# Two small tiles made larger in a one-core decoder layer, and the addresses that move with them

## The chip, the cores and the metric

The kernel runs on one core of a Trainium2 chip. A core has TensorE (matmuls, with a separate step that loads the stationary operand, called weights here), VectorE, ScalarE, GpSimd and SyncE, which work in parallel and wait for each other by semaphores, and 16 DMA engines. SBUF, its working memory, has 128 partitions; the address of a tile is its byte offset within each partition. PSUM takes the results of matmuls. The metric is the device time of one execution, in microseconds (us).

## The reference

One layer of a decoder on a sequence of 512 tokens of 1024 channels, in float32:

```python
cs = silu(c)
mod = cs @ w_ada + b_ada                 # six vectors of 1024
shift1, scale1, gate1, shift2, scale2, gate2 = split(mod)
h = rmsnorm(x, norm1_g) * (1 + scale1) + shift1
qa, ka, va, qd, kd, vd, ga, gd = split(h @ w_in)
out_a = sliding_window_attention(qa, ka, va)     # 8 heads, window 128, sinks
out_d = diff_attention(qd, kd, vd)               # 4 heads, two softmax maps each
merged = sigmoid(ga) * (out_a @ w_branch_swa) + sigmoid(gd) * (out_d @ w_branch_diff)
x = x + gate1 * (merged @ w_out)
h2 = rmsnorm(x, norm2_g) * (1 + scale2) + shift2
x = x + gate2 * conv_ffn(h2)                     # w_up, causal conv, GELU gate, w_down
out = rmsnorm(x, final_g)
```

## The kernel before

Every large product is made of three products in a reduced float32 format. An operand is split into a high part (a cast on ScalarE) and a low part (the rest, a subtraction on VectorE), and TensorE adds high × high, high × low and low × high into one PSUM bank. Where the weights are W and the other operand is h, a step is therefore Wh·hh, Wh·hl and Wl·hh; `mm3` (L131) issues these three. In the names of the profile a matmul reads as out<-moving,weights: `a<-hTA,w0h` has the weights w0h and moves hTA.

Tiles come from pools. A pool lays its buffers one behind another in the order in which the program first asks for them; a tag with `bufs=n` has n buffers in turn. A float32 tile of [128, N] takes 4N bytes of each partition, rounded up to 32. Pools that are closed give their space to the next ones, and a tile that is written over an older one's space waits for the last reader of that one.

Two stages are touched.

**The early loop** (`for gi in range(KT)`, L483, in manual order on VectorE, ScalarE and TensorE). It goes over the eight blocks k of 128 input channels. For each k it makes the modulation of the block (`ac_ops` and `ac_first` sum w_ada times cs on VectorE and ScalarE, `reduce_mod` sums over partitions on TensorE, L328, and `finish_mod` writes two columns into a small tile `mod`), then the normalised, transposed and modulated block hT (`h_turn`, `h_tile`, `h_low`), and `mm_k` (L396) adds the block to six PSUM banks: the first 768 columns of w_in, as 6 blocks of 128, times three products, 18 matmuls with 128x512 moving elements for each k. The third product (`part` 2, high weights, low hT) of k is issued behind the reduction and transposes for k + 1. The weights of the block, w0h and w0l, are tiles of [128, 768]. `split_hi` (L355) takes them from pool w for even k and from pool p1 for odd k:

```python
pl, nb = (wp, WB) if k % 2 == 0 else (pp, 2)
```

In pool p1 the last tiles asked for are, in order: three buffers of mod, two of hf, two of ac, two of w0h, and then two of w0l and two more of ac (ac's two parities have a tag each). mod has [128, 16], 64 bytes a buffer. With the sizes before, hf, ac and the odd weights begin 128 bytes past a multiple of 512. The weights of even k, in pool w, and those of all later projections (also pool w) begin at multiples of 512, and so does each block of 128 columns in them.

**The merge** (from L1096). `add_gate_d` computes the second gate of a block j of 128 channels (weights wgd, 8 × 3 matmuls), and `add_merge` the differential branch: w_branch_diff for two blocks at a time is loaded, split into the tile wbd (`gpart(3, ...)`, pool mlp), and 4 × 3 matmuls of 128x512 moving elements into bank pB use it. The units are queued as gate j, branch j − 1, and at the end branches 6 and 7 follow each other; then the output projection begins (`out_step`, L1452; its weights are the merged tiles mg, its moving tiles wo).

In pool mlp stand, in order: five buffers of gx and those of mg, tdall (buffer gT2), m2, c2, and behind c2 the buffers gT3 (wbd, then two weights of the up projection, then a row of the MLP's hidden activations), gT0 (normalised x, then others), gT1 (the same), gT4 (the first gate's row, then m5w, weights of one product of the up projection) and small statistics. c2 has [128, 40], 160 bytes. With the sizes before, everything behind it down to gT4 begins 160 bytes past a multiple of 512. c2 itself holds shift and scale of the second norm as columns: `turn_m2` (L1140) writes it, and the modulation of the second norm reads it.

Behind the merge come the output projection, the second norm, the up projection with convolution and GELU (L1390 and others) and the down projection (L2045), all with weights in pools w, big and the first tiles of mlp, but for m5w (24 matmuls with 256 moving columns) and the transposes of normalised x (L1496).

Of the kernel before, what the change touches and what calls it, by code (L numbers as in the profile page):

```python
# [8 lines left out]
F32 = mybir.dt.float32  # L9
# [5 lines left out]
P = 128  # L15
# [45 lines left out]
def kernel(  # L61
# [26 lines left out]
    def pool(name, bufs=1, space=None, stack=ctx):  # L88
        kw = {} if space is None else {"space": space}
        return stack.enter_context(tc.tile_pool(name=name, bufs=bufs, reuse_waits="tile", **kw))  # L90
# [128 lines left out]
    pp = pool("p1", stack=p1)  # L219
# [110 lines left out]

    def finish_mod(k, pa):
        pa = pa if k == 0 else [pa[:, 0], pa[:, 1]]
        m = pp.tile([P, 16], F32, tag="mod", bufs=3, name=f"mod{k}")
        last = nc.vector.scalar_tensor_tensor(
            m[:, 0:1], pa[0][:, 0:1], bsc1[:, k : k + 1], n1g[:, k : k + 1], ALU.add, ALU.mult
        )
        if k:
            nc.scalar.activation(m[:, 1:2], pa[1][:, 0:1], AF.Identity, bias=bsh[:, k : k + 1])
        else:
            nc.vector.tensor_add(m[:, 1:2], pa[1][:, 0:1], bsh[:, k : k + 1])  # L340
        mods[k] = m
        return last
# [131 lines left out]
    for j in range(2):  # L474
        nc.tensor.matmul(pa0[j], a0[j], ones, start=False, stop=True)
    turn(3)
    finish_mod(0, pa0)
    split_hi(0, 0)
    keep_warm(2)
# [3 lines left out]
    for gi in range(KT):  # L483
# [24 lines left out]
        if more:  # L508
            if gi == 0:
                split_lo(1, 0)  # L510
            pa = reduce_mod(gi + 1, early_mod(1) if gi == 0 else None)
            if gi == 0:
                mm_k(0, 0, FIRST[5:])
            if ALONE <= gi + 2 < KT:
                ac_first(gi + 2, 1)
                ac_first(gi + 2, 0)
            if gi:
                h_turn(gi + 1)
            last_mod = finish_mod(gi + 1, pa)
            if gi:  # L520
                split_lo(gi + 1, 0)
            split_lo(gi + 1, 1)
            h_tile(gi + 1)
# [572 lines left out]
    bp = pool("mlp")  # L1096
# [32 lines left out]
        units.append((load, branch))  # L1129

    m2 = bp.tile([40, P], F32, name="m2")
    c2 = bp.tile([P, 40], F32, name="c2")
    s2c, a2c = c2[:, 0:8], c2[:, 8:16]
    nc.sync.dma_start(m2[16:32, :], b_ada[0, 3 * D : 5 * D].rearrange("(a p) -> a p", p=P))
    nc.sync.dma_start(m2[32:40, :], norm2_g[0].rearrange("(a p) -> a p", p=P))
# [965 lines left out]
```

## Time and profile before

| | |
|---|---|
| median of 3 runs | 685.16 us (684.44 to 686.75) |
| the profiled execution | 685.38 us, of which the span of instructions is 683.6 |
| mean granted TensorE clock | 0.997 of full |
| early loop after k = 0, 19.3 to 55.5 us | TensorE busy 36.20 of 36.20 us, VectorE 33.34, ScalarE 26.41 |
| second gates and branches, 247 to 305 us | TensorE busy 58.00 of 58.00 us, VectorE 42.17, ScalarE 19.11 |
| TensorE's weight loads | 582.2 us, overlapping the matmuls |

In the profile's groups, a row has line, engine, operation, names, shapes and count, then busy time in us, the mean duration of one in ns, and the idle time before. In the view of one tile or line, a row has the count and then the least, the median and the largest duration in ns, and the first and last start in us. The timeline has start and duration in us. The end of a matmul is modelled by the profiler and overlaps the next one's start, so a duration of 0.39 us does not say that the next matmul starts 0.39 us later: the distance between starts does. Starts are shown to 0.01 us, so distances are best taken over many instructions.

### The profile page before, as it was taken

How to read it: one execution, taken by the hardware profiler on the slowest of the kernel's cores; microseconds unless marked ns; L12 is line 12 of the kernel's file. 1: busy time of each engine (PE TensorE's matmuls, PEld its weight loads, DVE VectorE, ACT ScalarE, POOL GpSimd, SP SyncE). 2: the span in 40 equal slices, each digit the busy share in tenths (PEclk: the TensorE clock that was granted, in tenths of full speed). 3: DMA queues.
4: the chain of work that ended last, by engine and by line, in shares of the span. 5: the costliest groups of instructions: out<-in, count | busy, mean ns of one | idle time of the engine just before them, and what ended most of it. 6: DMA issues, size and time to landing. Idle time of an engine off the chain costs nothing. (4 is left out here: it accounts for less than half of the span.)

```text
span 683.6 us, 10903 instructions
## 1 busy us (share of the span) xinstructions
PE 673.7 (99%) x4005; PEld 582.2 (85%) x4005; DVE 562.5 (82%) x1075; ACT 398.1 (58%) x722; POOL 98.4 (14%) x119
## 2 busy tenths in 40 slices
PE   8999999999999999999999999999999999999995
PEld 5887887878888888888899999999999998888885
DVE  4999875988796756794589988988888999979997
ACT  6776774546543223233377756666666776656765
POOL 3000000011022011021030101112111102440300
PEclk9999999999999999999999999999999999999998
DMA  9995422565466885469644788886879848995903
GB/s 304 351 301 175 144 62 65 161 167 163 142 159 179 254 245 164 163 187 340 204 89 108 174 195 206 185 184 190 213 163 217 207 146 203 201 204 144 167 1 123
DMA packets 117141, 123.87 MB, mean 181 GB/s; under 512 B 5063, under 2 KB 94184, under 8 KB 117088
## 3 DMA queue, kind: packets, MB, share of 16 engines
q1 hardware_dynamic: 97246, 95.11, 44.2%
q0 software_dynamic: 19648, 27.79, 24.3%
q8 instruction: 31, 0.51, 0.3%
q10 hardware_dynamic: 194, 0.28, 0.1%
q14 instruction: 22, 0.18, 0.1%
HBM read 118.97 MB, written 2.11 MB: 177 GB/s over the span
## 5 line engine op out<-in xcount | busy, mean ns | idle before, releaser
L1390 PE MATMUL up<-t,m_whi 128*128 128x256 f32 x512 | 93.5, 283 | 0.1
L1390 PEld LDWEIGHTS up<-t,m_whi 128*128 128x128 f32 x512 | 79.8, 192 | 0.8 <-ACT up L1427 0.3
L1390 PE MATMUL up<-t,m_wlo 128*128 128x256 f32 x256 | 72.4, 283 | 0.0
L953 POOL DMA_DIRECT2D arow<-arow x28 | 22.5, 802 | 249.1 <-DVE sd L822 123.2
L1390 PEld LDWEIGHTS up<-t,m_wlo 128*128 128x128 f32 x256 | 49.1, 192 | 0.0
L1373 PE MATMUL up<-bhl,p_whi 128*128 128x512 f32 x136 | 48.9, 399 | 0.0
L1272 POOL DMA_DIRECT2D s<-in_w_up_dram x21 | 26.9, 1352 | 144.2 <-DMA s<-in_w_up_dram 65.8
L1302 ACT CAST m_whi<-s 128x1024 fp32r<-128x1024 f32 x31 | 32.6, 1052 | 23.8 <-PE up L1390 10.3
L1306 DVE TENSOR_TENSOR m_wlo<-s,m_whi 128x1024 fp32r<-128x1024 f32 x31 | 37.9, 1221 | 6.0 <-ACT m_whi L1302 5.5
L945 DVE SCALAR_TENSOR_TENSOR arow<-ra,cs,arow 128x512 f32<-128x512 f32 x56 | 41.7, 747 | 0.6
L1377 PE MATMUL up<-bhl,p_wlo 128*128 128x256 f32 x136 | 38.3, 281 | 0.0
L1390 PE MATMUL up<-bhl,p_whi 128*128 128x256 f32 x192 | 35.1, 283 | 0.0
L1390 PE MATMUL up<-t,p_whi 128*128 128x256 f32 x176 | 32.1, 283 | 0.0
L1373 PEld LDWEIGHTS up<-bhl,p_whi 128*128 128x128 f32 x136 | 25.6, 188 | 5.5
L1390 PEld LDWEIGHTS up<-bhl,p_whi 128*128 128x128 f32 x192 | 30.0, 192 | 0.0
L817 ACT ACTIVATE sd<-sd,dmx 128x128 f32<-128x128 f32 (+3 forms) x32 | 17.7, 556 | 17.2 <-DVE dmx L807 17.2
L1390 PEld LDWEIGHTS up<-t,p_whi 128*128 128x128 f32 x176 | 27.4, 191 | 0.4
L1390 PE MATMUL up<-bhl,p_wlo 128*128 128x256 f32 x96 | 27.2, 283 | 0.0
L1377 PEld LDWEIGHTS up<-bhl,p_wlo 128*128 128x128 f32 x136 | 25.7, 189 | 0.0
L1390 PE MATMUL up<-t,p_wlo 128*128 128x256 f32 x88 | 24.9, 283 | 0.0
L1296 DVE TENSOR_TENSOR s<-s,wa 128x1024 f32<-128x1024 f32 x20 | 24.4, 1219 | 0.0
L1397 ACT ACTIVATE gT<-a,cv 128x512 f32<-128x512 f32 x22 | 17.8, 814 | 10.1 <-DVE a L1431 6.2
(501 smaller groups left out, 2085.6 us busy)
## 6 DMA issues: line engine op xcount, KB each, us to landing
ra<-in_w_ada_dram SPq DMA_DIRECT2D x32, 512.0 KB, 4.5
wa<-in_w_up_dram SPq DMA_DIRECT2D x22, 512.0 KB, 4.6
s<-in_w_up_dram SPq DMA_DIRECT2D x21, 512.0 KB, 5.6
s<-in_w_up_dram POOLq DMA_DIRECT2D x21, 512.0 KB, 7.3
w<-in_w_in_dram SPq DMA_DIRECT2D x12, 512.0 KB, 4.8
a<-in_w_up_dram SPq DMA_DIRECT2D x11, 512.0 KB, 4.2
b<-in_w_down_dram SPq DMA_DIRECT2D x10, 512.0 KB, 3.9
adaw<-in_w_ada_dram SPq DMA_DIRECT2D x8, 512.0 KB, 6.8
```

Source lines behind the costliest of these rows:

```text
L817: exp = nc.scalar.activation(pm[m], pm[m], AF.Exp, bias=mx[:, m : m + 1], scale=slope, accum_out=ls)
L945: nc.vector.scalar_tensor_tensor(ac, r[:, a], cc, ac, ALU.mult, ALU.add)
L953: nc.gpsimd.dma_start(whole[0:n], whole[n : 2 * n], accum_op=ALU.add)
L1272: nc.gpsimd.dma_start(dst, upblock(*blk), accum_op=ALU.add)
L1296: nc.vector.tensor_add(src, src, R[J, "a11" if name == "m6" else "a12"])
L1302: nc.scalar.copy(W[J, name][0], R[J, SRC[name]])
L1306: nc.vector.tensor_sub(lo, R[J, SRC[name]], hi.bitcast(F32))
L1373: nc.tensor.matmul(bk, wh[:, k, cu], bhl[:, i, k].rearrange("p b n -> p (b n)"), start=False, stop=k == 3, skip_group_check=True,)
L1377: nc.tensor.matmul(bk[:, :H], wl[:, k, cu], bhl[:, i, k, 0], start=False, stop=k == 3, skip_group_check=True)
L1390: nc.tensor.matmul(o[u], w[:, k, cu], b[:, k], start=opens and k == 0 and x == 0, stop=k == 3 and x == 2, skip_group_check=True,)
L1397: nc.scalar.activation(grow(j), av[J][:, u], AF.Identity, bias=cv[:, 66 + j : 67 + j], scale=cv[:, 44 + j : 45 + j])
```

## The change

The tile mod gets 48 columns in place of 16, 192 bytes a buffer in place of 64. c2 is now the first 40 columns of a tile with 128, 512 bytes in place of 160. The columns that are read and written stay the same, and no instruction is added or taken away. In p1 everything behind mod moves up by 384 bytes, to a multiple of 512; in mlp everything behind c2 moves up by 352 bytes, and the tiles down to gT4 come to multiples of 512.

```diff
     def finish_mod(k, pa):
         pa = pa if k == 0 else [pa[:, 0], pa[:, 1]]
-        m = pp.tile([P, 16], F32, tag="mod", bufs=3, name=f"mod{k}")
+        m = pp.tile([P, 48], F32, tag="mod", bufs=3, name=f"mod{k}")
...
     m2 = bp.tile([40, P], F32, name="m2")
-    c2 = bp.tile([P, 40], F32, name="c2")
+    c2 = bp.tile([P, P], F32, name="c2")[:, 0:40]
     s2c, a2c = c2[:, 0:8], c2[:, 8:16]
```

## The prediction

> **What bounds the kernel now.** I read the page's engine rows first, then its clock and DMA rows, and then who waited for whom on TensorE.
>
> ```profile
> span 683.6 us, 10903 instructions
> ...
> PE 673.7 (99%) x4005; PEld 582.2 (85%) x4005; DVE 562.5 (82%) x1075; ACT 398.1 (58%) x722; POOL 98.4 (14%) x119
> ...
> PEclk9999999999999999999999999999999999999998
> ```
>
> ```profile
> PE xt L433 <- DVE xn L425: 1.1, 1, 1.1
> PE a L184 <- POOL ones L143: 1.0, 1, 1.0
> PE pc L263 <- POOL ident masks.py:199: 0.2, 1, 0.2
> ```
>
> The second fence is the whole list of what the matmul stream waited for: 2.3 us, by lines that all run before the first projection. From then to the last matmul the stream has no wait worth listing, at a granted clock of 9 tenths or more until the last slice. So TensorE is the bound, and the time of a stage is its matmuls times the distance from one start to the next. A busy PE says nothing of that distance, because matmuls overlap; it has to be read from starts.
>
> The timeline (start, duration, engine, line, names) gives them. First the early loop, k=1 (first two rows) and k=2 (last two), whose weights are w0h and w0l:
>
> ```profile
> 21.53 0.40 PE L404 MATMUL a<-hTA,w0l 128*128 128x512 f32 x1
> ...
> 23.85 0.40 PE L404 MATMUL a<-hTA,w0l 128*128 128x512 f32 x1
> ...
> 26.57 0.39 PE L404 MATMUL a<-hTA,w0l 128*128 128x512 f32 x1
> ...
> 28.83 0.39 PE L404 MATMUL a<-hTA,w0l 128*128 128x512 f32 x1
> ```
>
> Between either pair lie ten distances, of the same instruction on the same moving tile hTA. The odd k takes 23.85 − 21.53 = 2.32 us, 0.232 each; the even k 28.83 − 26.57 = 2.26 us, 0.226 each. Nothing waits in either. What differs is where the weights lie: even k draw on pool w, at a multiple of 512 bytes, odd k on pool p1, 128 bytes past one.
>
> Now the merge: a gate's run (aligned weights wgd), the start of the gate behind a branch, and the last two branches (wbd, 160 bytes past a multiple):
>
> ```profile
> 276.93 0.39 PE L132 MATMUL pgd<-hTA,wgd_h 128*128 128x512 f32 x1
> ...
> 280.10 0.40 PE L134 MATMUL pgd<-hThB,wgd_l 128*128 128x512 f32 x1
> ...
> 291.77 0.40 PE L132 MATMUL pgd<-hTA,wgd_h 128*128 128x512 f32 x1
> 292.01 0.40 PE L133 MATMUL pgd<-hTA,wgd_h 128*128 128x512 f32 x1
> ...
> 293.62 0.39 PE L134 MATMUL pgd<-hTA,wgd_l 128*128 128x512 f32 x1
> ...
> 297.26 0.39 PE L132 MATMUL pB<-outdA,wbd 128*128 128x512 f32 x1
> ...
> 302.63 0.39 PE L134 MATMUL pB<-outdA,wbd 128*128 128x512 f32 x1
> ```
>
> The gate has 14 distances in 3.17 us, 0.2264 each. The branch has 23 in 5.37 us, 0.2335 each. The gate just behind a branch has its first 8 in 1.85 us, 0.2313 each: it takes eight matmuls for the stream to fall back into step.
>
> **The change part by part.** No instruction is added, removed or reordered; only addresses move. The three mod buffers grow by 128 bytes each, so what follows them in p1 (hf, ac, the odd w0h and w0l) moves by 384 bytes, from 128 past a multiple of 512 to one. c2 grows by 352, so what follows it in mlp (the buffers of gT3, gT0, gT1, gT4 and the small statistics) moves from 160 past to a multiple.
>
> *Odd first weights.* Four odd k with 6 channel blocks and 3 products make 72 weight loads. At 0.232 − 0.226 = 0.006 us each that is 0.43 us. Not all of it need reach the end, since in this loop VectorE is close behind:
>
> ```profile
> 28.58 0.43 DVE L302 TENSOR_TENSOR ac<-ac,ac 128x256 f32<-128x256 f32 x1
> ...
> 29.06 0.52 PEld L328 LDWEIGHTS pa<-ones,ac 128*128 128x128 f32 x4 [0.26 <-DVE ac L302]
> ...
> 33.27 0.42 DVE L302 TENSOR_TENSOR ac<-ac,ac 128x256 f32<-128x256 f32 x1
> ...
> 34.72 0.22 DVE L334 SCALAR_TENSOR_TENSOR mod<-pa,cols 128x1 f32<-128x1 f32 x1 [0.42 <-PE pa L328]
> ```
>
> At 29.06 us the reduction's weight load (L328) had waited 0.26 us for the vector sum that ended at 28.58 + 0.43 = 29.01. A TensorE that gets there earlier waits longer, so the gain of what stands before it, k=1 with its 18 loads (18 × 0.006 = 0.11 us), can be lost. One round later the sum ends at 33.69 us and it is VectorE that waits 0.42 us for TensorE: there 0.1 us of haste does no harm, because it is TensorE that sets the pace again. Bounds of this term: 0.32 us (all of k=1 lost) and 0.43. I take 0.35, near the lower end, since the row at 29.06 shows the wait.
>
> *Branch weights.* Eight branches of 4 × 3 matmuls are 96 loads: 96 × (0.2335 − 0.2264) = 0.68 us. Behind each run of branches stands one tail: six behind branches 0 to 5, one behind 6 and 7 together, where the output projection begins. At 8 × (0.2313 − 0.2264) = 0.04 us each, seven make 0.27 us. Together 0.95 us; I keep 0.68 (the tails have another cause) as the lower bound. No vector or DMA wait stands in the merge, so all of it is on the path.
>
> [...]
>
> *The other weights that move.* m5w is loaded under 256 moving columns:
>
> ```profile
> 361.46 3.04 PE L1390 MATMUL up<-t,m5w 128*128 128x256 f32 x24
> 364.33 0.40 PE L1390 MATMUL up<-t,m_whi 128*128 128x256 f32 x2
> ...
> L1390 PE MATMUL up<-t,m_whi 128*128 128x256 f32 x512 | 93.5, 283 | 0.1
> ...
> L1390 PE MATMUL up<-t,m5w x24: 278/281/286, 361.5 to 364.2; 128*128 128x256 f32 x24
> ```
>
> Its 24 take 364.33 − 361.46 = 2.87 us, 0.120 each, and a median of 281 ns stands against the 283 of aligned weights: they lose nothing, so I count 0 (bounds: 24 × ±0.006, ±0.14 us, if they behaved like the wide ones). The same holds for xn under the transposes of L1496 and for ac: no row shows a loss there.
>
> *Vector and scalar work on moved tiles.* L362 and L370 write even and odd weights alike, and L1397 writes gT2 and gT5 (at a multiple already) as well as the other four:
>
> ```profile
> L362 ACT CAST w0h<-w x8: 613/616/619, 13.7 to 46.6; 128x512 fp32r<-128x512 f32 x8
> L370 DVE TENSOR_TENSOR w0l<-w,w0h x8: 683/683/693, 14.7 to 49.8; 128x512 fp32r<-128x512 f32 x8
> L1397 ACT ACTIVATE gT<-a,cv x22: 800/816/823, 375.2 to 569.8; 128x512 f32<-128x512 f32 x22
> ```
>
> Half of each group is aligned and the extremes lie within 1 to 3%: no price for the address. I count 0; even a whole 1% of those writes would be hidden, both engines being off the path.
>
> *One new wait.* Moved by 352 bytes, wbd now reaches into the buffer where head 3's aTh lay in the attention pool, so its first write must wait for that head's last value product too.
>
> ```profile
> L134 PE MATMUL od<-aTh,qkv x16: 272/311/393, 136.2 to 205.9; 128*128 128x512 f32 x4, 128*128 128x384 f32 x4, 128*128 128x256 f32 x4, 128*128 128x128 f32 x4
> L128 ACT CAST wbd<-wbd x4: 1037/1049/1051, 235.2 to 292.7; 128x1024 fp32r<-128x1024 f32 x4
> ```
>
> The last read starts at 205.9 us, the first write at 235.2: 29 us of cover. Behind a late cast stand ScalarE's own casts and then branch 0, but nothing here can be 29 us late. Cost 0.
>
> Sum: 0.35 + 0.95 = 1.3 us, with 0.32 + 0.68 − 0.14 = 0.9 and 0.43 + 0.95 + 0.14 = 1.5 as its bounds. The profiled execution took 685.38 us (span 683.6, 1.8 around it) and becomes 684.1; the median of the runs shown, 685.16, is 0.22 below it, which gives **683.9 us**, 0.19% less. What is late next is TensorE again: outside the round at 29.06 nothing is near.
>
> **The rivals.** *The address isn't the cause.* The slow weights are also those that lie highest in memory, above everything in pool w, and no aligned weight under 512 moving columns lies quite as high. The groups by line and names (columns at the end: busy us, mean ns) have a neighbour, though:
>
> ```profile
> L132 PE MATMUL pB<-outdA,wbd 128*128 128x512 f32 x32 | 12.7, 398 | 0.0
> L1461 PE MATMUL oc<-wo_whi,mg3l 128*128 128x512 f32 x16 | 5.3, 389 | 0.0
> ```
>
> In the output projection the weights are mg's; mg3l lies at a multiple of 512, only some 13 KB below wbd in the same pool, and its matmuls last 389 ns where wbd's last 398. So height speaks weakly. By this rival the spacing stays at 0.232 and 0.2335 and the time at 685.2 us. [...] Chance 0.09.
>
> *Only one of the two goes.* The remainders differ, 128 and 160, and so do the patterns: tails stand behind wbd and hardly any behind odd k. If only the merge gains, 685.16 − 0.95 = 684.2; if only the early loop, 684.8. Chance 0.07.
>
> *Slower: loads and moving reads fall into step.* With weights and moving rows both at multiples of 512, a hidden load could meet the moving read at the same place each time. Its place is the 168 moved loads, and it decides as soon as their spacing passes what it is now. The slowest distance of the quoted rows is 292.01 − 291.77 = 0.24 us; if all took that, the cost would be 72 × 0.008 + 96 × 0.0065 = 1.2 us, so 686.4. Against it: the even k and the gates are in just that position and run at 0.226. Chance 0.04.
>
> **How the numbers follow.** The forecast (gain 0.9 to 1.5 us) has 0.80: alone it gives 683.7 to 684.3. But three runs of the kernel before lie between 684.44 and 686.75 us, so a median carries some 0.7 us either way, and the range is 682.5 to 685.7; it takes in the first two rivals and leaves out the third. About 0.3% (2.1 us) is what a measurement of this kernel can tell from no change, and the gain is below that. Passing it takes the forecast and a median 0.8 us further down, 0.14 in all. The slower rival by itself stays within 0.3%; with scatter on its side it gives 0.03. The remaining 0.83 is within 0.3%.
>
> **What would show it.** After, ten distances of an odd k should take 2.26 us like those of an even k; 23 of the last two branches 23 × 0.2264 = 5.21 us in place of 5.37; the gate behind a branch should start at 0.226 at once; the weight load of L328 at about 29 us should show a wait some 0.1 us longer; m5w and the casts stay; the span ends near 682.3. Odd k still at 0.232 makes the first rival right. A stretch outside these two stages that is longer, or a listed wait of TensorE behind 14 us, would show that the sum was incomplete.

## The result: 684.46 us, 0.94 us less, and where a part of the gain stayed

| | before | after |
|---|---|---|
| median | 685.4 us (22 runs, 684.44 to 686.83) | 684.46 us (22 runs, 21 of them between 683.24 and 686.03) |
| ratio of the runs | | 0.9986 [0.998, 0.9992] |
| profiled execution: span | 683.6 us | 683.5 us |
| mean granted clock | 0.997 | 0.997 |

One of the 22 executions of after took 949.86 us at a granted clock of 0.655, and the ratio leaves it out. The kernel is faster by 0.14%. The interval of the ratio does not reach 1, though the gain is within the 0.3% that the prediction counted as no change. The profiled execution of after, however, is only 0.1 us shorter than that of before, and it is the better teacher. The page's engine row and the list of what the matmul stream waited for:

```profile
span 683.5 us, 10903 instructions
...
PE 672.6 (98%) x4005; PEld 582.1 (85%) x4005; DVE 561.8 (82%) x1075; ACT 398.1 (58%) x722; POOL 98.5 (14%) x119
```

```profile
PE xt L433 <- DVE xn L425: 1.4, 1, 1.4
PE a L184 <- POOL ones L143: 1.0, 1, 1.0
PE pB L134 <- DVE wbd L129: 0.6, 1, 0.6
PE pc L263 <- POOL ident masks.py:199: 0.2, 1, 0.2
```

TensorE is 1.1 us less busy, and its list of waits has a new third row: a branch matmul waited 0.6 us for the low part of wbd.

First the distances, which did what was forecast. The timeline of after, odd k=1 (rows 1 and 2), branch 5 (3 and 4) and the gate behind it (5 and 6):

```profile
21.68 0.39 PE L404 MATMUL a<-hTA,w0l 128*128 128x512 f32 x1
...
23.95 0.39 PE L404 MATMUL a<-hTA,w0l 128*128 128x512 f32 x1
...
288.20 0.39 PE L132 MATMUL pB<-outdA,wbd 128*128 128x512 f32 x1
...
290.69 0.39 PE L134 MATMUL pB<-outdA,wbd 128*128 128x512 f32 x1
290.92 0.39 PE L132 MATMUL pgd<-hTA,wgd_h 128*128 128x512 f32 x1
...
292.73 0.39 PE L134 MATMUL pgd<-hTA,wgd_l 128*128 128x512 f32 x1
```

Ten distances of the odd k take 2.27 us (2.32 before), eleven of the branch 2.49 us, 0.2264 each (0.2335 before), and the first eight of the gate behind it 1.81 us (1.85 before): the tail is gone as well.

Now where it was given back. Setting each matmul of after beside the same one of before, and taking the difference of the two starts, gives this course:

| at (us of before) | after − before (us) | what happened in between |
|---|---|---|
| 10.6 | +0.13 | start-up, the same code |
| 21 | +0.17 | |
| 54.5 | −0.17 | early loop: −0.34 |
| 247 | −0.20 | −0.03, no single step |
| 297.3 | −0.90 | branches 0 to 5 and the gates behind them: −0.70 |
| 298.0 | −0.02 | branch 6: +0.88 in three matmuls |
| 304.7 | −0.16 | the rest of branches 6 and 7, and the first matmuls behind them: −0.14 |
| 345 | −0.02 | transposes of L1496: +0.14 |
| 676 | −0.08 | −0.06, no single step |

The start of branch 6 in the timeline of after:

```profile
296.36 0.39 PE L132 MATMUL pB<-outdA,wbd 128*128 128x512 f32 x1
296.58 0.39 PE L133 MATMUL pB<-outdB,wbd 128*128 128x512 f32 x1
297.60 0.50 PE L134 MATMUL pB<-outdA,wbd 128*128 128x512 f32 x1 [0.63 <-DVE wbd L129]
```

and of before:

```profile
297.73 0.39 PE L134 MATMUL pB<-outdA,wbd 128*128 128x512 f32 x1
```

The third matmul is the first that needs the low part. It starts at 297.60 where its two predecessors would have let it start at 296.81. Before, at 297.73, it was already just behind that low part. VectorE shows why, first after, then before (start, duration; the bracket is the idle time ahead and what ended it):

```profile
282.57 1.22 DVE L1195 TENSOR_TENSOR wo<-wo,g1b 128x1024 f32<-128x1024 f32 x1 [4.40 <-DMA wo<-in_w_out_dram]
...
296.33 1.22 DVE L129 TENSOR_TENSOR wbd<-wbd,wbd 128x1024 fp32r<-128x1024 f32 x1
```

```profile
282.59 1.23 DVE L1195 TENSOR_TENSOR wo<-wo,g1b 128x1024 f32<-128x1024 f32 x1 [3.80 <-DMA wo<-in_w_out_dram]
...
296.35 1.22 DVE L129 TENSOR_TENSOR wbd<-wbd,wbd 128x1024 fp32r<-128x1024 f32 x1
```

The low part ends at 297.55 us after and at 297.57 before. VectorE's time is the same because a transfer sets it: 4.40 us idle for the first block of w_out (3.80 before), then its work to the low part of wbd, in the order of the program. That transfer stands on SyncE's queue behind the modulation rows. SyncE's waits from 260 to 300 us after, its two issues after, and last POOL's idle time in the view of L953, after:

```profile
SPq L1138 <- DMA mod_rows<-arow: 9.9, 1, 9.9
```

```profile
276.69 0.33 SPq L1138 DMA_DIRECT2D m<-mod_rows  x1
277.12 0.38 SPq L1112 DMA_DIRECT2D wbd<-in_w_branch_diff_dram  x1
```

```profile
DMA arow<-arow: 86.2, 23
```

POOL sums the modulation rows by transfers that add into one another (L953), seven to a row; 23 times such a transfer waited for the one before it, 86.2 us in all. When the sums that L1138 reads have landed, SyncE issues it, after 9.9 us of waiting (before 10.1), and only behind it the loads of wbd and of w_out. A chain of transfers, with nothing of TensorE in it, ends just ahead of the matmul that needs its result; a TensorE that comes 0.9 us earlier waits.

The late issue is only a part of it, though. Before, SyncE issued the same transfers later still:

```profile
277.35 0.33 SPq L1138 DMA_DIRECT2D m<-mod_rows  x1
```

That is 0.66 us after the 276.69 of after, and yet VectorE got the first block of w_out at the same time (282.59 and 282.57). From the issue of L1138 to VectorE's use pass 5.24 us before and 5.88 after. With the 5.24 of before, the low part would have been ready in after at about 296.9 us, by an estimate from these rows, where TensorE wanted it at 296.81. So the wait of this execution came from a late chain and from a transfer that took 0.64 us longer; why it took longer is not known.

### The profile page after: what moved, and what is told of

The parts are those of the page before. It is cut to its first block, busy times and chain, and to the rows that moved or that the text cites. A ratio compares the mean times of both kernels' runs of the same rounds, so it can differ in the third digit from the quotient of the medians.

```text
span 683.5 us, 10903 instructions
## 1 busy us (share of the span) xinstructions
PE 672.6 (98%) x4005; PEld 582.1 (85%) x4005; DVE 561.8 (82%) x1075; ACT 398.1 (58%) x722; POOL 98.5 (14%) x119
## 3 DMA queue, kind: packets, MB, share of 16 engines
HBM read 118.97 MB, written 2.11 MB: 177 GB/s over the span
## 4 chain that ended last, share of the span: by engine, by line
PE 80%; DMA 11%; DVE 4%; issue 3%; POOL 1%; SPq 0%; ACT 0%; DVEq 0%; POOLq 0%; ACTq 0%
PE up L1390 25%; PE dc L2045 15%; DMA arow<-arow 7%; PE a L404 5%; PE up L1373 5%; PE up L1377 2%; PE oc L1457 2%; PE oc L1461 2%; PE oc L1458 2%; DMA adaw<-in_w_ada_dram 1%; DMA xn<-in_b_ada_dram 1%; PE pq L132 1%; PE sd L139 1%; PE pw L132 1%; PE pw L134 1%
## 5 line engine op out<-in xcount | busy, mean ns | idle before, releaser
L953 POOL DMA_DIRECT2D arow<-arow x28 | 22.5, 804 | 253.8 <-DVE sd L822 122.9
L1373 PE MATMUL up<-bhl,p_whi 128*128 128x512 f32 x136 | 48.9, 399 | 0.0
L1377 PE MATMUL up<-bhl,p_wlo 128*128 128x256 f32 x136 | 38.3, 281 | 0.0
L1373 PEld LDWEIGHTS up<-bhl,p_whi 128*128 128x128 f32 x136 | 25.6, 188 | 5.5
L1377 PEld LDWEIGHTS up<-bhl,p_wlo 128*128 128x128 f32 x136 | 25.7, 189 | 0.0
L1397 ACT ACTIVATE gT<-a,cv 128x512 f32<-128x512 f32 x22 | 17.8, 814 | 10.1 <-DVE a L1431 6.2
```

The lines of the kernel that those rows point to most:

```text
L953: nc.gpsimd.dma_start(whole[0:n], whole[n : 2 * n], accum_op=ALU.add)
L1373: nc.tensor.matmul(bk, wh[:, k, cu], bhl[:, i, k].rearrange("p b n -> p (b n)"), start=False, stop=k == 3, skip_group_check=True,)
L1377: nc.tensor.matmul(bk[:, :H], wl[:, k, cu], bhl[:, i, k, 0], start=False, stop=k == 3, skip_group_check=True)
L1397: nc.scalar.activation(grow(j), av[J][:, u], AF.Identity, bias=cv[:, 66 + j : 67 + j], scale=cv[:, 44 + j : 45 + j])
```

## Experiments

The theory that the comparison leaves: the address costs what the distances say, in both places; and the late low part of wbd takes the merge's gain back whenever the chain of transfers is late. Its rivals: the two parts don't add up; the gain has another cause than the address; or the wait isn't what keeps the total small, so that VectorE's order changes nothing. Each expectation names the theories that it sets against each other.

### One part alone

Only the first line of the change:

```diff
-        m = pp.tile([P, 16], F32, tag="mod", bufs=3, name=f"mod{k}")
+        m = pp.tile([P, 48], F32, tag="mod", bufs=3, name=f"mod{k}")
```

> Only mod is made larger; wbd stays 160 bytes past a multiple of 512. Theory A (both stages start their matmuls faster, but most of the merge's gain is handed back at branch 6, which waits for VectorE's low part of wbd): the early loop ends 0.36 us earlier, the merge keeps its distance of 0.2335 us, branch 6 waits for nothing, ratio to before about 0.9995 (-0.35 us). Theory B (the gain of both stages passes through to the end, and the 0.94 us measured is simply 0.35 + 0.6): the same for this kernel, 0.9995. Theory C (what matters isn't the address of the weights): early loop unchanged at 0.232 us, ratio 1.0000.

Only the second:

```diff
-    c2 = bp.tile([P, 40], F32, name="c2")
+    c2 = bp.tile([P, P], F32, name="c2")[:, 0:40]
```

> Only c2 is made larger; the odd weights stay 128 bytes past a multiple of 512. Theory A: the early loop keeps 0.232 us; the branches start every 0.227 us, TensorE is 0.7 us earlier at branch 6 and then waits 0.5 to 0.8 us for the low part of wbd; net -0.2 to -0.4 us, ratio 0.9994 to 0.9997. Theory B: no such wait, -0.6 to -0.9 us, ratio 0.9987 to 0.9991.

| | median (11 runs; before 685.52 of 33) | ratio | mean distance, odd k | mean distance in pB | shift of TensorE in its stage (one execution) |
|---|---|---|---|---|---|
| mod alone | 685.04 us | 0.9994 [0.9985, 1.0003] | 227.3 ns | 233.5 ns | −0.24 us, early loop |
| c2 alone | 684.89 us | 0.9994 [0.9984, 1.0003] | 232.5 ns | 226.9 ns | −0.91 us, merge |

(Mean distances here and below are over all starts of such matmuls that follow each other without a gap. Before they are 232.5 for odd k, 227.8 for even k and 233.5 in pB; after 227.5, 228.6 and 227.4.) Each edit cures its own distances and leaves the other's alone. As times, neither can be told from before by these intervals. The table's last column, a shift within one execution, shows what the medians can't tell. With c2 alone the wait at branch 6 was expected and did not come: in that execution SyncE issued L1138 at 274.87 us instead of 276.69, the low part was done at 295.31, TensorE needed it at 297.27, and the whole 0.91 us of the merge stayed. So the wait is not a fixed consequence of the change.

### VectorE's order: the low part of wbd ahead of the later products of w_out

The last wbd's low part is put before the gate products of L1195 for k from 3 on, with the change and without it:

```diff
-                    split(wh, wl, r)
+                    pair_w["low"] = split(wh, wl, r)[1]
...
-        with tc.issue_after(paced[-1].ins) if k == KT - 1 else ExitStack():
+        with tc.issue_after((paced[-1] if k == KT - 1 else pair_w["low"]).ins) if k > 2 else ExitStack():
```

> The changed kernel, and VectorE is told to make the low part of the last wbd before it scales wo for k = 3 and later, some 1.5 us sooner than now. Theory A: the wait of branch 6 for wbd is gone, TensorE keeps its 0.9 us there, ratio to before 0.9978 to 0.9983 (-1.2 to -1.5 us), that is 0.3 to 0.6 us under the changed kernel. Theory B: as the changed kernel, 0.9986.

> The kernel before with the same order on VectorE. Theory A: there the low part of wbd comes just in time already (it ends at 297.57 us, and the matmul that needs it starts at 297.73), so the order alone brings at most 0.1 us, ratio 0.9998 to 1.0001. A rival to the reading of e3 (the order is worth something by itself, whatever the addresses): the same 0.3 to 0.6 us as between e3 and the changed kernel, ratio 0.9991 to 0.9996.

In another job, on another chip, the kernel after as it is and the new order with the change once more:

> The changed kernel once more, beside e6 on the same chip. Theory A (the wait at branch 6 comes in some executions and not in others, by when the chain of transfers that ends in the modulation rows is through): 0.998 to 0.999, and a profile in which the low part of the last wbd ends either before 296.9 us (then no wait, and branches start every 0.227 us through to the end) or after it (then a wait). Theory A' (the wait is always there): a wait of 0.5 us or more again.

> The changed kernel with VectorE's new order (as e3), once more beside e5. Theory A: 0.2 to 0.7 us under e5, ratio to before 0.9974 to 0.9984; a rival, that the order is worth nothing and e3 was scatter: the time of e5.

| | median (11 runs) | ratio to before of the same job | wait at branch 6 in the profile |
|---|---|---|---|
| new order, with the change | 684.0 us | 0.9979 [0.9971, 0.9988] | none |
| new order, without it | 685.56 us | 0.9999 [0.999, 1.0008] | none |
| after, again | 683.97 us | 0.9979 [0.9969, 0.999] | none |
| new order, with the change, again | 685.39 us | 0.9993 [0.998, 1.0006] | none |

The first job alone would have told a neat story: the order costs nothing by itself and lifts the gain to the whole sum. The second takes it back: the kernel after as it is has the same 0.9979, and the new order has 0.9993. The profile of the last run has a wait that no other shows: in the early loop, near 51 us, a matmul waited 0.9 us for a cast of the block hThB. So the worth of the new order is not shown, and no version here is shown to beat after.

What the second run of after does show is the change without the wait. Its branch 6, VectorE's low part, and SyncE's wait, in three views:

```profile
295.33 0.39 PE L132 MATMUL pB<-outdA,wbd 128*128 128x512 f32 x1
295.56 0.39 PE L133 MATMUL pB<-outdB,wbd 128*128 128x512 f32 x1
295.78 0.39 PE L134 MATMUL pB<-outdA,wbd 128*128 128x512 f32 x1
```

```profile
291.93 1.22 DVE L129 TENSOR_TENSOR wbd<-wbd,wbd 128x1024 fp32r<-128x1024 f32 x1
```

```profile
SPq L1138 <- DMA mod_rows<-arow: 5.9, 1, 5.9
```

SyncE waited 5.9 us in place of 9.9, the low part was done at 293.15, 2.6 us ahead of its use, and the three matmuls follow each other at 0.225. The shift between this execution and the one of before, at two ends, is read from the same instruction in both. Before:

```profile
10.62 0.33 PE L433 MATMUL xt<-ident,xn 128*128 128x128 f32 x1 [1.09 <-DVE xn L425]
...
303.56 0.39 PE L1458 MATMUL oc<-wo_wlo,mg0h 128*128 128x512 f32 x1
```

After, second run:

```profile
9.84 0.33 PE L433 MATMUL xt<-ident,xn 128*128 128x128 f32 x1 [0.48 <-DVE xn L425]
...
301.45 0.39 PE L1458 MATMUL oc<-wo_wlo,mg0h 128*128 128x512 f32 x1
```

At 10.6 us, before anything of the change has run, this execution is 0.78 us ahead by its start-up alone; at 303.6 it is 2.11 ahead. The change is the difference, 1.33 us, against a forecast of 1.3. Some 0.15 us of it goes again at the transposes of L1496, so that 1.2 us reach the end (at 676 us this execution is 1.98 us ahead).

### Other remainders

Is it 512, or some smaller unit? The two tiles are given other widths, so that the odd weights and wbd come to other remainders:

```diff
-        m = pp.tile([P, 16], F32, tag="mod", bufs=3, name=f"mod{k}")
+        m = pp.tile([P, 112], F32, tag="mod", bufs=3, name=f"mod{k}")
...
-    c2 = bp.tile([P, 40], F32, name="c2")
+    c2 = bp.tile([P, 144], F32, name="c2")[:, 0:40]
```

The others differ in the two widths alone: 96 and 64, 8 and 96, 32 and 160.

> mod with 112 columns and c2 with 144: the odd first weights begin 256 bytes past a multiple of 512, wbd 64 bytes past. If only multiples of 512 are free of loss: odd k 0.230 to 0.234 us from start to start, branches 0.230 to 0.236. If a multiple of 64 were enough, branches 0.2267; if 256 were enough, odd k 0.2267.

> mod with 96 columns and c2 with 64: the odd first weights begin 64 bytes past a multiple of 512, wbd 256 bytes past. If only multiples of 512 are free of loss: both 0.230 to 0.236 us from start to start. If 64 (or 256) were enough, the stage with that remainder at 0.2267.

> mod with 8 columns and c2 with 96: the odd first weights begin 32 bytes past a multiple of 512, wbd 384 bytes past (so neither at a multiple of 256). If multiples of 256 are what is free of loss: odd k 0.232 us from start to start, branches 0.233. If it is enough for wbd to be a multiple of 128: branches 0.227.

> mod with 32 columns and c2 with 160: the odd first weights begin 320 bytes past a multiple of 512 (64 past one of 256), wbd 128 bytes past. If multiples of 256 are what is free of loss: odd k 0.233, branches 0.233 us. If a remainder of 128 costs less in the merge than 160 does: branches between 0.227 and 0.233.

| widths of mod, c2 | odd weights: bytes past a multiple of 512, mean distance | wbd: the same | time, one run |
|---|---|---|---|
| 16, 40 (before) | 128: 232.5 ns | 160: 233.5 ns | |
| 48, 128 (after) | 0: 227.5 | 0: 227.4 | |
| 112, 144 | 256: 227.4 | 64: 233.5 | 684.96 us |
| 96, 64 | 64: 233.0 | 256: 227.1 | 684.44 |
| 8, 96 | 32: 232.7 | 384: 232.9 | 684.71 |
| 32, 160 | 320: 233.1 | 128: 233.0 | 685.05 |

The view of tile wbd has it in one row each (least, median and largest duration in ns, first and last start). Before, then widths 112 and 144, 96 and 64, 8 and 96, in this order:

```profile
L133 PE MATMUL pB<-outdB,wbd x32: 392/399/399, 247.4 to 302.4; 128*128 128x512 f32 x32
```

```profile
L133 PE MATMUL pB<-outdB,wbd x32: 392/396/398, 247.0 to 301.9; 128*128 128x512 f32 x32
```

```profile
L133 PE MATMUL pB<-outdB,wbd x32: 388/389/393, 246.5 to 301.4; 128*128 128x512 f32 x32
```

```profile
L133 PE MATMUL pB<-outdB,wbd x32: 389/394/405, 246.9 to 301.8; 128*128 128x512 f32 x32
```

Only the third, with wbd at remainder 256, has the median of 389 ns that aligned weights have; 160, 64 and 384 have 394 to 399. A multiple of 256 bytes was enough in both places (227.4 ns for odd k, 227.1 for wbd), and no gradation was seen: each of the other remainders tried (32, 64, 128, 160, 320, 384) costs 5 to 6.5 ns a matmul. The tails behind them do differ. With the odd weights at 64, 32 and 320, the even k too, whose own weights did not move, take 229.9, 229.6 and 230.3 ns, where with 128 they take 227.8: the first seven or so matmuls of each are slow, as behind the branches. The widths 96 and 64 also had a wait of 0.46 us at branch 6. Of the four profiled executions with the cured wbd and VectorE's old order (after twice, c2 alone, and this one) two have the wait.

One rival is not separated by these runs, nor by those of the next section. In every slow group one of the two tiles of the matmul, weights or moving, lay at a multiple of 512, and the other did not lie at a multiple of 256. Whether each tile's own address counts, or only that the two remainders differ, would need both tiles shifted alike, and that was not tried.

### The dose: all of pool w

If 168 loads at a bad address cost 1.3 us, then shifting everything that lies in pool w should cost several times that. A pad goes ahead of the pool's split weights, and a second behind them, so that what follows moves up by 512 bytes and keeps its remainder:

```diff
-    man = ExitStack()
+    man, pad = ExitStack(), wp.tile([P, 32], F32, name="pad")
...
-    keep_warm(2)
+    keep_warm(2); fill2 = wp.tile([P, 96], F32, name="pad2")
```

This shifts by 128 bytes; with 64 columns in both pads it is 256.

> The kernel before, with 128 unused bytes ahead of the split weights of pool w and 384 behind them: all those weights now begin 128 bytes past a multiple of 512, and the other pools keep their remainders. 840 matmuls with 512 moving columns load such weights (288 of the heads, 384 of the gates, 96 of the sliding-window branch, 72 of even k), and 136 more in the up projection. Theory (the remainder costs 0.005 to 0.0066 us for each such matmul, wherever the tile lies): 840 of them make +4.2 to +5.5 us, with the 136 up to +6.4, ratio 1.006 to 1.0095, and even k at 0.232 us. Rival (only the high pools are sensitive): 1.0000.

> The same with 256 unused bytes ahead and 256 behind: all split weights of pool w begin 256 bytes past a multiple of 512. Theory (multiples of 256 are enough): 0.9995 to 1.0005, even k at 0.228 us as in the kernel before. Rival (512 is needed here, and e7 was special to its pool): as e11.

| shift of pool w | median | ratio (before 685.29, 13 runs) | even k | second gates |
|---|---|---|---|---|
| 128 bytes | 689.61 us (4 runs) | 1.0063 [1.0046, 1.008] | 232.3 ns | 232.9 ns |
| 256 bytes | 685.26 us (10 runs) | 0.9997 [0.9987, 1.0006] | 228.5 | 227.9 |

The same added bytes cost 4.3 us at one remainder and nothing at the other. The timeline of gate matmuls, shifted by 128 bytes:

```profile
278.05 0.40 PE L132 MATMUL pgd<-hTA,wgd_h 128*128 128x512 f32 x1
...
279.92 0.40 PE L134 MATMUL pgd<-hTA,wgd_l 128*128 128x512 f32 x1
```

and by 256:

```profile
277.19 0.39 PE L132 MATMUL pgd<-hTA,wgd_h 128*128 128x512 f32 x1
...
279.01 0.39 PE L134 MATMUL pgd<-hTA,wgd_l 128*128 128x512 f32 x1
```

Eight distances take 1.87 us in the first and 1.82 in the second. The 4.3 us aren't spread evenly, though. The view by line gives the first and last start (after the three durations) in the output, up and down projections; before:

```profile
L1457 PE MATMUL oc<-wo_whi,mg0h x16: 389/389/397, 302.9 to 312.9; 128*128 128x512 f32 x16
...
L1390 PE MATMUL up<-t,m_whi x512: 278/283/385, 364.3 to 565.2; 128*128 128x256 f32 x171
...
L2045 PE MATMUL dc<-m5wh,m5a x44: 389/389/389, 586.2 to 600.9; 128*128 128x512 f32 x44
```

Shifted by 128 bytes:

```profile
L1457 PE MATMUL oc<-wo_whi,mg0h x16: 390/393/404, 305.7 to 315.9; 128*128 128x512 f32 x16
...
L1390 PE MATMUL up<-t,m_whi x512: 274/281/385, 368.2 to 567.0; 128*128 128x256 f32 x171
...
L2045 PE MATMUL dc<-m5wh,m5a x44: 390/393/404, 588.3 to 603.4; 128*128 128x512 f32 x44
```

In L1457 and L2045 the tile of pool w is the moving one (wo_whi, m5wh) and the weights (mg0h, m5a) lie in pool mlp, where nothing moved: 10.0 us become 10.2, and 14.7 become 15.1. So a bad address of the moving tile costs too. In the up projection, weights of pool w stand under 256 moving columns, and there the shift *gains*: 200.9 us become 198.8. By the differences of starts, the shifted kernel loses 3.1 us up to 297 us, 1.0 more to the end of the output projection, gains 2.06 in the up projection and loses 2.47 in the down projection: 4.5 in all, of which the span shows 4.3 (687.9 against 683.6) because its start-up was 0.24 us ahead.

That the total lies in the forecast of 4.2 to 6.4 us is in part luck. That forecast was for weights alone. The 840 matmuls with such weights have all run by 297 us, and the 3.1 us lost until then are 3.7 ns for each, less than the 5 to 6.6 of the theory: second gates go from 228 to 233 ns, but most of the heads' matmuls began at 227 to 230 and end at 231 to 233. The losses by moving tiles (1.0 and 2.47 us) and the gain in the up projection were not forecast. The 136 matmuls of the up projection with 512 moving columns (L1373, weights p_whi in pool w) even go against the theory: from their start to the next one's, the mean falls from 236.6 to 231.3 ns. Each has a matmul with 256 columns behind it (L1377), and the pair goes from 354.0 to 351.5 ns.

## Why the prediction was right, and the step that failed

Forecast 683.9 us with a range of 682.5 to 685.7; measured 684.46, and 683.97 in the second job. The range is wide enough to hold the time of before as well (685.16 in the prediction, 685.4 here), so that the time lies in it says little. What bears the prediction out are the distances.

- **The bound** was read rightly: where nothing waits, time is matmuls times the distance of starts, and the change moved those distances.
- **Odd first weights**, 0.35 us: shown. The early loop gains 0.34 us in both executions of after. With mod alone it was 0.24 in the one execution profiled, below the lower bound of 0.32. There the gain of k = 1 was lost at the reduction near 24 us, one round earlier than the one that the prediction named: the weight load of L328 waited 0.27 us there (0.19 before, and not at all in either execution of after). The profile names nothing that it waited for.
- **The round at 29 us**: the wait of L328's load was to be some 0.1 us longer. It is 0.27 us against 0.26, since VectorE's sum itself came 0.06 us later (28.64 us against 28.58). The observation did not show what was forecast, and the term held all the same.
- **Branch weights**, 0.95 us, tails included: shown. It is 0.91 us in the second execution of after (−1.22 to −2.13) and 0.91 with c2 alone. By mean distances, 96 × (0.2335 − 0.2269) = 0.63 us are the loads and 192 × (0.2279 − 0.2267) = 0.23 the tails in the gates.
- **"No vector or DMA wait stands in the merge, so all of it is on the path", and "outside the round at 29.06 nothing is near"**: this step failed. The low part of wbd for branches 6 and 7 ended 0.16 us ahead of its use before (297.57 against 297.73). I read only what the matmuls waited for. The list of the weight loads' waits in the profile of before had the warning, a small one:

```profile
PEld pB L134 <- DVE wbd L129: 0.2, 1, 0.2
```

and after it has grown:

```profile
PEld pB L134 <- DVE wbd L129: 1.1, 1, 1.1
```

  In executions in which the chain of transfers and the first block of w_out are late, up to 0.9 us of the 1.3 go there; in others, none. That fits a median gain of 0.94 us in one job and 1.33 in the other, but in how many of the timed runs the wait occurred was not seen, so its share in those medians is argued, not shown.
- **xn under the transposes of L1496**, 0: off by 0.14 us. The weight load of the first transpose waits for xn a little longer (0.30 us in place of 0.17). It is not simply a faster TensorE: with wbd and xn at remainder 64, where the merge gained nothing, the wait is as long, and with 128 it is as before. Why stays open.
- **m5w**, casts and subtractions, the new wait of wbd on head 3: 0, as forecast. m5w's mean distance is 120.0 ns against 119.6, and L370 lasts 682 ns against 683.
- **The rivals.** That the address isn't the cause falls with remainder 256: wbd and the odd weights then lie elsewhere and still lose nothing, while 32, 64, 128, 160, 320 and 384 cost 5 to 6.5 ns a matmul. That only one of the two goes falls with the runs of one part alone. Against the slower one, loads and moving reads falling into step, are the distances measured at multiples of 512 (227.5 ns for odd k and 227.4 in pB, in after).
- **Multiples of 512**, on which the prediction's terms were put, are more than is needed: 256 does as well, as the odd weights (227.4 ns), wbd (227.1) and pool w (228.5 for even k, 227.9 in the second gates) showed once each.

## What to carry to other kernels

Where TensorE is the bound, compare distances of starts between groups of the same shape; a group that is 2 to 3% slower without a wait may be a matter of its tiles' addresses. Here a multiple of 256 bytes cured it for weights under 512 moving columns (from 232.5 and 233.5 ns to 227.4 and 227.1), and cost nothing for moving tiles (220.3 ns in the down projection, as before); this leaves out the up projection with its mixture of 256 and 512 columns. Before counting a gain as whole, go through the waits of the weight loads too and, for each later use, compare when the operand was ready with when it was needed: the 0.16 us here was gone as soon as TensorE came 0.9 us earlier. And an order that looks better by 0.1% in one job has to be seen in another before it is believed.

## What the runs showed of the hardware

- In the early loop and the merge a 512-column matmul took 227 to 229 ns from start to start, on average, with its tiles at multiples of 256 bytes, and 232 to 233.5 with its weights at any other remainder tried (32, 64, 128, 160, 320, 384). Behind a group of such weights the first seven or eight matmuls were slow too (before, 231.3 ns each in the gate behind branch 5), so that even k came to 229.6 to 230.3 ns where the odd weights were at 64, 32 and 320. The 512-column matmuls of the up projection, which alternate with 256-column ones, don't follow this (236.6 ns, and 231.3 with the weights shifted by 128 bytes).
- The recorded duration of wbd's weight loads does not show it: a median of 188 ns in before (remainder 160) and after (0) alike. The matmuls' distances do: 233.5 and 227.4 ns.
- The moving tile's address cost much the same: in the down projection, shifting it by 128 bytes raised the mean distance from 220.3 to 225.4 ns (476 distances, some of them of 256 columns); shifted by 256 bytes it is 220.3 again.
- Under 256 moving columns it was the other way: with weights off a multiple of 256 the mean distance fell from 120.2 to 118.7 ns (m_whi, 512 distances), some 2 us over the up projection. m5w (24 matmuls), with weights at remainder 160 before and at a multiple of 512 after, shows next to nothing of it: 119.6 and 120.0 ns. No run here says why.
- The chain of adding transfers ended at different times from execution to execution: SyncE issued L1138 at 271.67 us in the second run of after, at 276.69 in the first and at 277.35 in before.
